# Hybrid decoder step on one core: key-norm reciprocals as a power on GpSimd, output blocks of 96, 96 and 72 rows

## The chip, the cores and the metric

The kernel runs on one core of one Trainium2 chip. The metric is the device time of one execution in microseconds (us). The engines are TensorE (PE in the profile, its weight loads PEld), VectorE (DVE), ScalarE (ACT), GpSimd (POOL) and SyncE (SP), which here only starts transfers. Transfers start on the queues of SP and of ACT.

## The reference

One layer of a hybrid decoder, for 256 new prompt positions and 8 decoding samples, 264 columns in all, in float32:

```
x = x + 0.5 * swiglu(rmsnorm(x, n1), f1g, f1u, f1d)
proj = rmsnorm(x, nm) @ w_in
mixed = [window attention with sinks and relative bias | RWKV-7 time mixing]
x = x + mixed @ w_out
x = x + 0.5 * swiglu(rmsnorm(x, n2), f2g, f2u, f2d)
y = rmsnorm(x, final_norm)
```

The model width is 2048, the feed-forward width 5504. The RWKV half has 16 heads of 64. In it, each head's key direction is normalised before the scan over time:

```
kk = k * k_k
kk = kk / max(sqrt(sum(kk * kk over the head)), 1e-12)
```

It also returns the window keys and values, the RWKV state and the shift columns of both kinds of sequence.

## The kernel before

**Layout.** Activations lie with 128 model columns on the partitions and the 264 sequence columns on the free axis, so x is 16 blocks of 128x264. Weights come from memory in chunks of 128x512 or 128x384.

**The split product.** Every weight product (`gemm`, lines 144 to 158) is made in three passes of a reduced float32 form: `chunk` (133 to 142) loads a chunk into `raw` (six buffers, SP's queue), ScalarE writes its rounded part `hi` (line 140), VectorE the rest, `lo = raw - hi` (line 141, through the helper on line 67), each in a ring of four. For each of the chunk's blocks TensorE makes hi x hi, hi x lo and lo x hi. TensorE thus waits for a chunk's `hi` and `lo`, and ScalarE and VectorE wait for a free place in the ring.

**Stages.** `first_ffn` (312), then `mixing` (363), then `second_ffn` (996). In the mixing stage the input projection's blocks run in the order of SEQ (line 48). Each RWKV pair of heads (eight pairs, two to a batch) spawns a generator `prep` (437), each batch a generator `chain` (562), each attention block `attend`; `tick` (91) advances all of them once after every chunk of a product, and `pause(n)` lets n ticks go by. So the small work of the mixing stage is interleaved with the big products in the program's order. The framework then orders each engine's instructions with a planner that prices each instruction and keeps a timeline (`schedule_with_timeline_sim=True`, line 1181); on the chip each engine takes its own instructions in that order.

**The norm of the keys** (447 to 464). `kk` is the scaled key of a pair (128 partitions, two heads), `b` its square. After `pause(PW[0])` a product with `bo`, a matrix of ones over each head's 64 partitions, sums the squares into PSUM, `nps`. VectorE takes the reciprocal of `nps` into `b` (453). Then come the scan of the decays (455), GpSimd's memset of the first column of `W` (456), the exponentials, a copy to `wc`, and after `pause(PW[1])` one VectorE operation makes `b = min(b, 1e24) * kk` (463). From `b` follow the pair's operands `BK` and `XD`, and with them the batch's chain.

**The end** (1028 to 1072). The last product's squares are summed over the model axis. y is written in two forms. Blocks 0 to 7 and 12 to 15 go out as they lie, 128 partitions by 264 columns each, into `yT`, after a product with the reciprocal root spread over all partitions. Blocks 8 to 11 are turned by TensorE, so that the 264 sequence positions lie on partitions in three groups of 88 rows, 512 wide; ScalarE and VectorE scale them by a reciprocal root per row (`rt`) and they go into `yt`. `sums`, `turns` and `spread` are TensorE's parts, held in the order of the program. The stores of `yt` are two on SP and one on ACT; of `yT` three on SP and two on ACT.

Of the kernel before, what the change touches and what calls it, by code (L numbers as in the profile page):

```python
# [7 lines left out]
F32 = mybir.dt.float32  # L8
F32R = mybir.dt.float32r
AF = mybir.ActivationFunctionType  # L10
ALU = mybir.AluOpType
AX = mybir.AxisListType

P = 128
NP = 256
NB = 8
T = NP + NB
D = 2048
# [24 lines left out]
PX = (1, 2, 1, 1)  # L43
DL = 2
XA = 3
ALPHA = math.exp(-0.5)
LKV = 26
SEQ = [('b', 0), ('b', 1), ('b', 2), ('kv', 0), ('kv', 1), ('kv', 2), ('kv', 3), ('q', 0), ('q', 1), ('q', 2), ('q', 3), ('b', 3), ('q', 4), ('q', 5), ('q', 6), ('q', 7)]
# [7 lines left out]
def body(tc, I, O):  # L56
    nc = tc.nc
    V, A, G, TE, SP = nc.vector, nc.scalar, nc.gpsimd, nc.tensor, nc.sync
# [7 lines left out]
    def tt(e, out, a, b, op):  # L66
        return e.tensor_tensor(out=out, in0=a, in1=b, op=op)  # L67
# [4 lines left out]
    def ts(e, out, a, s1, op0, s2=None, op1=None):  # L72
        k = {} if op1 is None else dict(op1=op1)
        e.tensor_scalar(out=out, in0=a, scalar1=s1, scalar2=s2, op0=op0, **k)

    def act(out, in_, f, **k):
        return A.activation(out=out, in_=in_, func=f, **k)  # L77

    def bc(ap, shape):
        return ap.broadcast_to(list(shape))  # L80

    def mm(out, lhsT, rhs, start=True, stop=True, **k):
        return TE.matmul(out, lhsT, rhs, start=start, stop=stop, **k)  # L83
# [24 lines left out]
    with ExitStack() as ctx:  # L108
        cp = ctx.enter_context(tc.tile_pool(name="cp", bufs=1))
# [52 lines left out]
        ss = cp.tile([P, NSH, NB], F32, name="ss")  # L162
        ones = cp.tile([P, P], F32, name="ones")
        G.memset(ones, 1.0)
        eps = cp.tile([P, 2], F32, name="eps")
        G.memset(eps[:, 0:1], 1e-5)
        G.memset(eps[:, 1:2], 64e-5)
        act(eps[:, 0:1], eps[:, 0:1], AF.Copy)
# [199 lines left out]
        def mixing_body(mx, n2, n3, XD, XR):  # L368
# [11 lines left out]
            ident, bo, cm = C[:, CID:CID + P], C[:, CBO:CBO + P], C[:, CCM:CCM + P]  # L380
            msk = C[:, CMK:CMK + P]
            keep = fix((P, NP), "keep")
# [54 lines left out]
            def prep(p, bt, k, xrr, xk, xv):  # L437
# [9 lines left out]
                kk, b = tmp(), tmp()  # L447
# [2 lines left out]
                yield from pause(PW[0])  # L450
                nps = mp()
                mm(nps[:, :T], bo, b)
                V.reciprocal(b, nps[:, :T])
                W, Wi = tmp((P, 4, 65)), tmp((P, 4, 64))
                V.tensor_tensor_scan(Wi.rearrange("p c t -> p (c t)"), keep, sg[:, :NP], 0.0, ALU.mult, ALU.add)
                G.memset(W[:, :, 0:1], 1.0)
                act(W[:, :, 1:65], Wi, AF.Exp, scale=-ALPHA)
                act(Wi, Wi, AF.Exp, scale=ALPHA)
# [24 lines left out]
                vp = mp()  # L483
# [18 lines left out]
                for c in range(4):  # L502
                    for h in range(2):
                        r = HALF[h]
                        mm(gps[h][:, c * P:(c + 1) * P], BK[r, c, h:h + 2, :], KR[r, 0:2, c, :])
                for h in range(2):
# [3 lines left out]
                    for blk in range(2):  # L510
                        x = blk * 32
# [6 lines left out]
                kp = mp()  # L518
# [17 lines left out]
                for i in range(NB):  # L536
                    c, g = i // 2, i % 2
                    for h in range(2):
                        r, o = HALF[h], HALF[1 - h]
# [371 lines left out]
            for kind, i in SEQ:  # L911
                if kind == "b":
                    bt = newbatch(i)
                    for k in range(BATCH[i]):
                        p = bt.p0 + k
                        x = [shifted(2 + 3 * p + j, tmp()) for j in range(3)]
# [5 lines left out]
                elif kind == "kv":  # L922
                    w, p = i // 2, i % 2
# [11 lines left out]
                else:  # L935
                    ps = win(LKV + 4 + i)
                    q = ob[i]
# [8 lines left out]
            xr = blk("x1", 8) + blk("x0", 8)  # L946
            for o in range(XA):
                SP.dma_start(xr[o], xsp[o])
# [15 lines left out]
            for pi, ks in enumerate(PASS):  # L964
# [3 lines left out]
                to = pairs(*(late + [xs4[1], more] if ks[0] > 7 else xs4[:1]))  # L968
# [11 lines left out]
                for o in range(KD):  # L980
                    if not pi and o + XA < KD:
                        behind(SP.dma_start(xr[o + XA], xsp[o + XA]))
                    ps = acc()
# [12 lines left out]
        def second_ffn(n3, xr, XR):  # L996
            fin = Norm(VGF, most=3)

            def load(k):
                if k >= CH:  # L1000
                    n3.split(xr[k], True)

            with tc.tile_pool(name="f2", bufs=1) as fp:
                cur[0] = (fp, NH)
                ys = [fp.tile([P, 4, T], F32, tag="y", bufs=4, name=uid("y")) for _ in range(4)]
                rt = fp.tile([88, 48], F32, name="rt")
                sq = fp.tile([P, NQ, T], F32, name="sq")
                n3.sq = fin.sq = [sq[:, j] for j in range(NQ)]

                def nxt(o):  # L1010
                    fin.square(xr[o])
                    if o == 0:
                        act(rt[:, 7:8], fin.sums[0][0][0:88, 0:1], AF.Sqrt)
                    act(ys[o // 4][:, o % 4], xr[o], AF.Copy, scale=vc(VGF + o))

                def last(ps, x):
                    a, b = slice(0, 176), slice(176, T)
                    q = fin.free.pop(0)
                    u, w = fin.sums[0]
                    tt(G, w, w, u, ALU.add)  # L1020
                    stt(x[:, a], ps[:, a], 0.5, x[:, a], ALU.mult, ALU.add)
                    stt(x[:, b], ps[:, b], 0.5, x[:, b], ALU.mult, ALU.add)
                    tt(V, q[:, b], x[:, b], x[:, b], ALU.mult)
                    act(q[:, a], x[:, a], AF.Square)
                    fin.sums[0] = [w, q]
                    act(ys[3][:, 3], x, AF.Copy, scale=vc(VGF + KD - 1))

                side = dec_state(fp, XR)
                ffn(n3, xr, I["gu2"], I["dn2"], nxt, load, None, side, end=last)
                assert next(side, side) is side  # L1030
                p, ident = fin.sums[0], C[:, CID:CID + P]
                assert len(p) == 2
                sm, rp, again = mp(), mp(), acc()
                turn, keep = [mp(), acc(), mp()], tc.keep_in_program_order
                todo = [(j, o) for j in range(3) for o in range(4)]

                def sums(i):
                    for j in range(3):
                        keep(mm(sm[0:88, j:j + 1], p[i][:, j * 88:j * 88 + 88], ones[:, 0:1], i + j == 0, i == 1, skip_group_check=True))

                def turns(n):
                    for _ in range(n):
                        j, o = todo.pop(0)
                        keep(TE.transpose(turn[j][0:88, o * P:o * P + P], ys[2][:, o, j * 88:j * 88 + 88], ident))

                def spread(to):
                    for j in range(3):
                        keep(TE.transpose(to[:, j * 88:j * 88 + 88], bc(rt[:, j:j + 1], (88, P)), ident[0:88, 0:88]))

                sums(0)  # L1050
                turns(5)
                sums(1)
                act(rt[:, 0:3], sm[0:88, 0:3], AF.Sqrt, scale=1.0 / D, bias=eps[0:88, 0:1])
                V.reciprocal(rt[:, 0:3], rt[:, 0:3])
                yt = fp.tile([88, 3, 512], F32, name="yt")
                rb = tmp()
                turns(4)
                spread(again)
                spread(rp)
                turns(3)  # L1060
                act(yt[:, 0], turn[0][0:88, :], AF.Copy, scale=rt[:, 0:1])
                ts(V, yt[:, 1], turn[1][0:88, :], rt[:, 1:2], ALU.mult)
                SP.dma_start(O["yt"][:, 0], yt[:, 0])
                SP.dma_start(O["yt"][:, 1], yt[:, 1])
                A.copy(rb, again[:, :T])
                act(yt[:, 2], turn[2][0:88, :], AF.Copy, scale=rt[:, 2:3])
                A.dma_start(O["yt"][:, 2], yt[:, 2])
                for e, q, o, n, d, r in ((V, SP, 0, 1, 0, rp[:, :T]), (V, SP, 1, 3, 1, rp[:, :T]), (G, A, 4, 3, 4, rb),
                                         (V, SP, 12, 4, 8, rp[:, :T]), (V, A, 7, 1, 7, rp[:, :T])):
                    y = ys[o // 4][:, o % 4:o % 4 + n]  # L1070
                    tt(e, y, y, bc(r.unsqueeze(1), (P, n, T)), ALU.mult)
                    q.dma_start(O["yT"][:, d:d + n, :], y)

        xsp = [dp.tile([P, T], F32, tag=f"xsp{o}", name=f"xsp{o}") for o in range(KD)]
# [4 lines left out]
        with tc.tile_pool(name="dx", bufs=1) as dx:  # L1079
# [2 lines left out]
            second_ffn(n3, mixing(n2, n3, XD, XR), XR)  # L1082


OUTS = dict(yT=(P, 12, T), yt=(88, 3, 512), kp=(2, P, P), vp=(2, P, P), ks=(NB, P, 256), vs=(NB, P, 256),
            wkvp=(NPAIR, P, 64), wkvs=(P, 64, 64), sh=(P, NSH, NB + 1))


# [69 lines left out]

def unlay(o):
    y = o["yT"].transpose(2, 1, 0).reshape(T, 12 * P)  # L1160
    y = np.concatenate([y[:, :8 * P], o["yt"].transpose(1, 0, 2).reshape(T, 512), y[:, 8 * P:]], 1)
    kv = lambda x: np.ascontiguousarray(x.reshape(2, 2, 64, P).transpose(3, 0, 1, 2)).reshape(1, 1, P, 4, 64)
    wp = o["wkvp"].reshape(16, 64, 64).transpose(0, 2, 1)[None, None]
    ws = o["wkvs"].reshape(2, 8, NB, 64, 64).transpose(2, 1, 0, 3, 4).reshape(1, NB, 16, 64, 64)
    sh = np.empty((9, NSH * P), np.float32)
    sh[:, _sources()[:NSH * P] - 1536] = o["sh"].transpose(2, 1, 0).reshape(9, NSH * P)
    c = np.ascontiguousarray
    return (c(y[None, :NP]), c(y[NP:, None]), kv(o["kp"]), kv(o["vp"]), c(wp), c(sh[None, None, 0]),
            c(o["ks"].reshape(1, NB, P, 4, 64)), c(o["vs"].reshape(1, NB, P, 4, 64)), c(ws), c(sh[None, 1:]))
# [15 lines left out]
```

## Time and profile before

| | |
|---|---|
| median of 3 runs | 1936.75 us (1935.41 to 1936.86) |
| the profiled execution's own time | 1936.05 us |
| its span, first to last instruction | 1934.2 us |
| TensorE busy | 1920.2 us, 99% |
| VectorE busy | 1311.8 us, 68% |
| ScalarE busy | 1027.9 us, 53% |
| GpSimd busy | 258.2 us, 13% |
| bytes moved | 357.28 MB, mean 185 GB/s |
| granted TensorE clock, mean | 0.999 |

The page of a profile lists the busy time of each engine, the chain of work that ended last (each step followed back to what released it), and groups of equal instructions: line, engine, operation, output and inputs, shape, count, then busy time, mean duration in ns, and the engine's idle time just before them with what ended it. A view by windows gives each engine's busy time in a stretch, with the number of instructions in brackets, and then the granted clock, the share of the 16 DMA engines' time and GB/s. A timeline has start, duration, engine and instruction; rows of the same kind that follow each other are merged, with their count. Line 67 is the helper for two-input operations, line 70 for operations with a scalar and a tensor, line 74 for operations with scalars, line 77 for ScalarE's functions, line 83 for products; so groups are told apart by the names of their tiles.

### The profile page before, as it was taken

The numbers are of one execution on the slowest core, as the hardware profiler recorded it, in microseconds if no ns is written. First come the engines' busy times: TensorE is split into PE (matmuls) and PEld (weight loads), VectorE is DVE, ScalarE is ACT, GpSimd is POOL, SyncE is SP. The second block draws the span as 40 slices with busy tenths as digits, with TensorE's granted clock in tenths as the row PEclk, the third lists the DMA queues.
The fourth block names the chain that finished last, engine by engine and source line by source line (L and its number), as shares of the span: only waits on it lengthen the run. The fifth ranks groups of instructions, "written<-read, shape, count | busy, mean of one in ns | idle before, by whom it ended". The sixth has DMA issues, their size and how long they took to land.

```text
span 1934.2 us, 45549 instructions
## 1 busy us (share of the span) xinstructions
PE 1920.2 (99%) x17171; PEld 1896.7 (98%) x17171; DVE 1311.8 (68%) x2622; ACT 1027.9 (53%) x2041; POOL 258.2 (13%) x376
## 2 busy tenths in 40 slices
PE   9999999999999999999999999999999999999998
PEld 9999999999999999999989999999999999999997
DVE  5865555655556568889888977866666666666655
ACT  5644444444444457676667555644444444444446
POOL 0401101011010113222101100300101001010012
PEclk9999999999999999999999999999999999999999
DMA  7566666665666668655645756666666666666664
GB/s 241 177 192 196 185 195 194 184 191 176 191 183 181 186 183 241 173 165 156 173 124 159 211 155 184 175 188 188 188 195 194 185 193 189 195 195 185 192 181 149
DMA packets 218599, 357.28 MB, mean 185 GB/s; under 512 B 33522, under 2 KB 71938, under 8 KB 218378
## 3 DMA queue, kind: packets, MB, share of 16 engines
q1 hardware_dynamic: 212054, 346.39, 61.0%
q10 hardware_dynamic: 6323, 7.98, 1.3%
q8 instruction: 134, 2.20, 0.5%
q14 instruction: 88, 0.71, 0.1%
HBM read 346.67 MB, written 9.69 MB: 184 GB/s over the span
## 4 chain that ended last, share of the span: by engine, by line
PE 98%; ACT 1%; DVE 0%; DMA 0%; issue 0%; DVEq 0%
PE acc L83 90%; PE m L83 7%; DMA x<-in_x 0%; ACT hi L140 0%; ACT t L77 0%; ACT BT L532 0%; ACT kr L523 0%; PE m L527 0%; PE m L808 0%; PE m L485 0%; DVE y L67 0%; PE m L728 0%; ACT x L953 0%; PE m L809 0%; PE m L810 0%
## 5 line engine op out<-in xcount | busy, mean ns | idle before, releaser
L67 DVE TENSOR_TENSOR lo<-raw,hi 128x512 fp32r<-128x512 f32 (+1 forms) x1288 | 875.3, 683 | 512.2 <-ACT hi L140 490.3
L140 ACT CAST hi<-raw 128x512 fp32r<-128x512 f32 (+1 forms) x1288 | 777.0, 606 | 815.9 <-PE acc L83 742.7
L83 PE MATMUL acc<-x,hi 128*128 128x264 f32 x4840 | 894.5, 286 | 1.0 <-ACT hi L140 1.0
L83 PEld LDWEIGHTS acc<-x,hi 128*128 128x128 f32 x4840 | 750.3, 189 | 6.3 <-issue 2.5
L83 PE MATMUL acc<-x,lo 128*128 128x264 f32 x2420 | 690.8, 286 | 0.2 <-DVE lo L67 0.2
L83 PE MATMUL acc<-h,hi 128*128 128x264 f32 x2752 | 495.0, 284 | 0.0
L83 PEld LDWEIGHTS acc<-x,lo 128*128 128x128 f32 x2420 | 457.2, 189 | 2.2 <-DVE lo L67 0.6
L83 PEld LDWEIGHTS acc<-h,hi 128*128 128x128 f32 x2752 | 424.4, 189 | 0.0
L83 PE MATMUL acc<-h,lo 128*128 128x264 f32 x1376 | 387.8, 284 | 0.0
L83 PEld LDWEIGHTS acc<-h,lo 128*128 128x128 f32 x1376 | 259.2, 189 | 0.0
L67 POOL TENSOR_TENSOR t<-t,t 128x264 f32<-128x264 f32 x74 | 79.9, 1079 | 1096.0 <-DVE t L67 949.8
L83 PE MATMUL acc<-y,hi 128*128 128x264 f32 x648 | 122.7, 284 | 0.0
L83 PE MATMUL acc<-o,hi 128*128 128x264 f32 x648 | 120.1, 284 | 0.0
L83 PE MATMUL acc<-kv,hi 128*128 128x264 f32 x582 | 109.7, 285 | 0.0
L83 PEld LDWEIGHTS acc<-y,hi 128*128 128x128 f32 x648 | 101.2, 189 | 0.1
L83 PEld LDWEIGHTS acc<-o,hi 128*128 128x128 f32 x648 | 100.1, 189 | 0.0
L70 DVE SCALAR_TENSOR_TENSOR x<-acc,x 128x264 f32<-128x264 f32 (+1 forms) x193 | 81.2, 425 | 24.3 <-PE acc L83 23.4
L83 PE MATMUL acc<-y,lo 128*128 128x264 f32 x324 | 92.0, 284 | 0.0
L83 PE MATMUL acc<-o,lo 128*128 128x264 f32 x324 | 92.0, 284 | 0.0
L83 PEld LDWEIGHTS acc<-kv,hi 128*128 128x128 f32 x582 | 89.9, 189 | 0.1
L67 DVE TENSOR_TENSOR t<-acc,t 128x264 f32<-128x264 f32 x156 | 67.4, 432 | 32.8 <-PE acc L83 32.8
L83 PE MATMUL acc<-kv,lo 128*128 128x264 f32 x291 | 82.9, 285 | 0.0
(309 smaller groups left out, 1596.1 us busy)
## 6 DMA issues: line engine op xcount, KB each, us to landing
raw<-in_gu SPq DMA_DIRECT2D x688, 256.0 KB, 3.3
raw<-in_dn SPq DMA_DIRECT2D x224, 256.0 KB, 2.8
raw<-in_win SPq DMA_DIRECT2D x152, 256.0 KB, 3.5
raw<-in_dn SPq DMA_DIRECT2D x160, 192.0 KB, 2.7
raw<-in_wout SPq DMA_DIRECT2D x64, 256.0 KB, 3.5
xsp<-x ACTq DMA_DIRECT2D x16, 132.0 KB, 3.9
x<-xsp SPq DMA_DIRECT2D x16, 132.0 KB, 4.5
ld<-in_sT SPq DMA_DIRECT2D x16, 128.0 KB, 3.1
```

What stands on the lines that cost most here:

```text
L67: return e.tensor_tensor(out=out, in0=a, in1=b, op=op)
L70: return V.scalar_tensor_tensor(out=out, in0=a, scalar=s, in1=b, op0=op0, op1=op1)
L83: return TE.matmul(out, lhsT, rhs, start=start, stop=stop, **k)
L140: A.copy(hi[:, :w], raw[:, :w])
```

## The change

The reciprocal of the summed squares is no longer taken by VectorE from PSUM. ScalarE copies the sums out of PSUM into `b`, and GpSimd raises `b` to the power of minus one, element by element, with the exponent read from a third column of `eps` that is spread over the 264 columns. The third column is set once at the start, by a memset on GpSimd.

At the end, the turned blocks are cut into groups of 96, 96 and 72 rows in place of three of 88. The root and the reciprocal per row are made in two steps, one for the first two groups and one for the third. `yt` in memory becomes 264 x 512. The fully laid out blocks are stored as 0, 1 to 3, 4 to 7 and 12 to 15 in place of 0, 1 to 3, 4 to 6, 12 to 15 and 7; GpSimd multiplies blocks 4 to 7, four of them. Queues: SP has the first two row groups, block 0 and blocks 4 to 7; ACT has the third row group, blocks 1 to 3 and 12 to 15.

```diff
+ROWS = ((0, 96), (96, 96), (192, 72))
...
-        eps = cp.tile([P, 2], F32, name="eps")
+        eps = cp.tile([P, 3], F32, name="eps")
+        G.memset(eps[:, 2:3], -1.0)
...
                 mm(nps[:, :T], bo, b)
-                V.reciprocal(b, nps[:, :T])
+                A.copy(b, nps[:, :T])
+                tt(G, b, b, bc(eps[:, 2:3], (P, T)), ALU.pow)
...
                 def spread(to):
-                    for j in range(3):
-                        keep(TE.transpose(to[:, j * 88:j * 88 + 88], bc(rt[:, j:j + 1], (88, P)), ident[0:88, 0:88]))
+                    for j, (c, n) in enumerate(ROWS):
+                        keep(TE.transpose(to[:, c:c + n], bc(rt[0:n, j:j + 1], (n, P)), ident[0:n, 0:n]))
...
-                act(rt[:, 0:3], sm[0:88, 0:3], AF.Sqrt, scale=1.0 / D, bias=eps[0:88, 0:1])
-                V.reciprocal(rt[:, 0:3], rt[:, 0:3])
-                yt = fp.tile([88, 3, 512], F32, name="yt")
+                for c, n in ((slice(0, 2), ROWS[0][1]), (slice(2, 3), ROWS[2][1])):
+                    act(rt[0:n, c], sm[0:n, c], AF.Sqrt, scale=1.0 / D, bias=eps[0:n, 0:1])
+                    V.reciprocal(rt[0:n, c], rt[0:n, c])
+                yt = fp.tile([P, 3, 512], F32, name="yt")
...
-                for e, q, o, n, d, r in ((V, SP, 0, 1, 0, rp[:, :T]), (V, SP, 1, 3, 1, rp[:, :T]), (G, A, 4, 3, 4, rb),
-                                         (V, SP, 12, 4, 8, rp[:, :T]), (V, A, 7, 1, 7, rp[:, :T])):
+                for e, q, o, n, r in ((V, SP, 0, 1, rp[:, :T]), (V, A, 1, 3, rp[:, :T]), (G, SP, 4, 4, rb), (V, A, 12, 4, rp[:, :T])):
                     y = ys[o // 4][:, o % 4:o % 4 + n]
                     tt(e, y, y, bc(r.unsqueeze(1), (P, n, T)), ALU.mult)
+                    d = min(o, 8)
                     q.dma_start(O["yT"][:, d:d + n, :], y)
```

`sums` and `turns` take their groups of rows from ROWS in the same way.

More of the change, by code (lines that the diff above doesn't have):

```diff
@@ L1005, in second_ffn @@
                 ys = [fp.tile([P, 4, T], F32, tag="y", bufs=4, name=uid("y")) for _ in range(4)]
-                rt = fp.tile([88, 48], F32, name="rt")
+                rt = fp.tile([P, 48], F32, name="rt")
                 sq = fp.tile([P, NQ, T], F32, name="sq")
@@ L1012, in nxt @@
                     if o == 0:
-                        act(rt[:, 7:8], fin.sums[0][0][0:88, 0:1], AF.Sqrt)
+                        act(rt[:, 7:8], fin.sums[0][0][:, 0:1], AF.Sqrt)
                     act(ys[o // 4][:, o % 4], xr[o], AF.Copy, scale=vc(VGF + o))
@@ L1037, in sums, with turns @@
                 def sums(i):
-                    for j in range(3):
-                        keep(mm(sm[0:88, j:j + 1], p[i][:, j * 88:j * 88 + 88], ones[:, 0:1], i + j == 0, i == 1, skip_group_check=True))
-                def turns(n):
-                    for _ in range(n):
+                    for j, (c, n) in enumerate(ROWS):
+                        keep(mm(sm[0:n, j:j + 1], p[i][:, c:c + n], ones[:, 0:1], i + j == 0, i == 1, skip_group_check=True))
+                def turns(k):
+                    for _ in range(k):
                         j, o = todo.pop(0)
-                        keep(TE.transpose(turn[j][0:88, o * P:o * P + P], ys[2][:, o, j * 88:j * 88 + 88], ident))
+                        c, n = ROWS[j]
+                        keep(TE.transpose(turn[j][0:n, o * P:o * P + P], ys[2][:, o, c:c + n], ident))
                 def spread(to):
-                    for j in range(3):
-                        keep(TE.transpose(to[:, j * 88:j * 88 + 88], bc(rt[:, j:j + 1], (88, P)), ident[0:88, 0:88]))
+                    for j, (c, n) in enumerate(ROWS):
+                        keep(TE.transpose(to[:, c:c + n], bc(rt[0:n, j:j + 1], (n, P)), ident[0:n, 0:n]))
                 sums(0)
@@ L1060, in second_ffn @@
                 turns(3)
[L1061 to L1064, printed above, removed]
+                ends = [(rt[0:n, j:j + 1], turn[j][0:n, :], yt[0:n, j], O["yt"][c:c + n]) for j, (c, n) in enumerate(ROWS)]
+                r, x, y, o = ends[0]
+                act(y, x, AF.Copy, scale=r)
+                SP.dma_start(o, y)
+                r, x, y, o = ends[1]
+                ts(V, y, x, r, ALU.mult)
+                SP.dma_start(o, y)
                 A.copy(rb, again[:, :T])
-                act(yt[:, 2], turn[2][0:88, :], AF.Copy, scale=rt[:, 2:3])
-                A.dma_start(O["yt"][:, 2], yt[:, 2])
-                for e, q, o, n, d, r in ((V, SP, 0, 1, 0, rp[:, :T]), (V, SP, 1, 3, 1, rp[:, :T]), (G, A, 4, 3, 4, rb),
-                                         (V, SP, 12, 4, 8, rp[:, :T]), (V, A, 7, 1, 7, rp[:, :T])):
+                r, x, y, o = ends[2]
+                act(y, x, AF.Copy, scale=r)
+                A.dma_start(o, y)
+                for e, q, o, n, r in ((V, SP, 0, 1, rp[:, :T]), (V, A, 1, 3, rp[:, :T]), (G, SP, 4, 4, rb), (V, A, 12, 4, rp[:, :T])):
                     y = ys[o // 4][:, o % 4:o % 4 + n]
                     tt(e, y, y, bc(r.unsqueeze(1), (P, n, T)), ALU.mult)
+                    d = min(o, 8)
                     q.dma_start(O["yT"][:, d:d + n, :], y)
@@ L1082, in body @@
             second_ffn(n3, mixing(n2, n3, XD, XR), XR)
-OUTS = dict(yT=(P, 12, T), yt=(88, 3, 512), kp=(2, P, P), vp=(2, P, P), ks=(NB, P, 256), vs=(NB, P, 256),
+OUTS = dict(yT=(P, 12, T), yt=(T, 512), kp=(2, P, P), vp=(2, P, P), ks=(NB, P, 256), vs=(NB, P, 256),
             wkvp=(NPAIR, P, 64), wkvs=(P, 64, 64), sh=(P, NSH, NB + 1))
@@ L1160, in unlay @@
     y = o["yT"].transpose(2, 1, 0).reshape(T, 12 * P)
-    y = np.concatenate([y[:, :8 * P], o["yt"].transpose(1, 0, 2).reshape(T, 512), y[:, 8 * P:]], 1)
+    y = np.concatenate([y[:, :8 * P], o["yt"], y[:, 8 * P:]], 1)
     kv = lambda x: np.ascontiguousarray(x.reshape(2, 2, 64, P).transpose(3, 0, 1, 2)).reshape(1, 1, P, 4, 64)
```

## The prediction

> **What bounds the kernel now.** I read the page's engine shares first, then the chain of work that ended last, then the costliest groups.
>
> ```profile
> span 1934.2 us, 45549 instructions
> PE 1920.2 (99%) x17171; PEld 1896.7 (98%) x17171; DVE 1311.8 (68%) x2622; ACT 1027.9 (53%) x2041; POOL 258.2 (13%) x376
> PE 98%; ACT 1%; DVE 0%; DMA 0%; issue 0%; DVEq 0%
> L67 DVE TENSOR_TENSOR lo<-raw,hi 128x512 fp32r<-128x512 f32 (+1 forms) x1288 | 875.3, 683 | 512.2 <-ACT hi L140 490.3
> L140 ACT CAST hi<-raw 128x512 fp32r<-128x512 f32 (+1 forms) x1288 | 777.0, 606 | 815.9 <-PE acc L83 742.7
> ```
>
> TensorE is the bound: it is busy for 1920.2 of 1934.2 us and holds 98% of the chain. ScalarE (`hi`) and VectorE (`lo`) split each weight chunk for it, and the 742.7 us in which ScalarE waits for TensorE to give back a chunk say that the split normally runs ahead. The change lies in two other places: in the mixing stage, where the key norms are made, and in the stores of the end. So next come the window of the eight pairs, and the line of the reciprocal.
>
> ```profile
> core 0: us, PE busy (x) PEld busy (x) DVE busy (x) ACT busy (x) POOL busy (x), PEclk, DMA share, GB/s
> 785.00:1050.00 265.00, 262.97 (x3063) 247.91 (x3063) 234.75 (x658) 173.52 (x445) 51.87 (x129) 1.00 0.56 157
> L453 DVE RECIPROCAL t<-m x8: 1794/1795/1808, 787.4 to 1036.2; 128x264 f32<-128x264 f32 x8
> ```
>
> Even here TensorE is idle for only 265.00 - 262.97 = 2.0 us, at a full granted clock. VectorE is the second engine: 234.75 of 265 us, 89%. GpSimd has room on average, 51.87 us.
>
> **The change part by part, the reciprocal first.** It removes 8 reciprocals of 1.80 us from VectorE, 14.4 us. Did they cost TensorE anything? The timelines of VectorE and of TensorE around the first:
>
> ```profile
> 786.52 0.69 DVE L67 TENSOR_TENSOR lo<-raw,hi 128x512 fp32r<-128x512 f32 x1
> 787.40 1.81 DVE L453 RECIPROCAL t<-m 128x264 f32<-128x264 f32 x1 [0.18 <-PE m L83]
> 789.41 0.68 DVE L67 TENSOR_TENSOR lo<-raw,hi 128x512 fp32r<-128x512 f32 x1
> 790.00 0.43 DVE L70 SCALAR_TENSOR_TENSOR t<-t,t 128x264 f32<-128x264 f32 x1
> 787.32 0.41 PE L83 MATMUL acc<-x,hi 128*128 128x264 f32 x2
> 787.68 0.41 PE L83 MATMUL acc<-x,hi 128*128 128x264 f32 x2
> 788.06 0.40 PE L83 MATMUL acc<-x,hi 128*128 128x264 f32 x2
> 788.42 0.40 PE L83 MATMUL acc<-x,hi 128*128 128x264 f32 x2
> ```
>
> During the reciprocal TensorE starts a group of three products every 0.36 to 0.38 us, without a gap. The ring of four `hi`/`lo` chunks covers it: a chunk is four such groups, 4 x 0.36 = 1.44 us. Removing the reciprocal is therefore worth nothing on the path; the most that all of this stage could give back is the 2.0 us above.
>
> In its place come a ScalarE copy out of PSUM and a power on GpSimd, on 128x264. The nearest rows:
>
> ```profile
> L77 ACT ACTIVATE t<-m 128x264 f32<-128x264 f32 x8 | 3.2, 400 | 1.0 <-PE m L83 1.0
> ACT hi L140 <- PE acc L83: 44.0, 46, 3.1
> L67 POOL TENSOR_TENSOR t<-t,t 128x264 f32<-128x264 f32 x74 | 79.9, 1079 | 1096.0 <-DVE t L67 949.8 <-ACT hi L140 123.4 <-ACT t L77 20.8
> L74 POOL TENSOR_SCALAR t<-t 128x264 f32<-128x264 f32 x8 | 4.0, 502 | 16.8 <-ACT t L77 16.8
> L74 POOL TENSOR_SCALAR XD<-t 128x8 f32<-128x8 f32 x8 | 2.5, 307 | 2.2 <-ACT t L77 1.8 <-DMA ld<-in_bias 0.3
> L460 POOL COPY wc<-t 128x4 f32<-128x4 f32 x8 | 3.2, 402 | 7.7 <-ACT t L77 7.7
> ```
>
> The copy: 8 x 0.40 = 3.2 us of ScalarE, hidden by the 44.0 us that it waits for TensorE (second row, between 780 and 1050 us). I set it to nothing; without that cover it would be 3.2 us. While it waits for the norm's matmul, `hi` casts stand behind it on ScalarE, as `lo` subtractions stood behind the reciprocal before.
>
> The power: no row shows one. **Bounds.** Below: 1.08 us, what GpSimd takes for a plain two-input operation of this size (from there the change is free). Above: the dearest price per column that GpSimd shows, 402 ns for 4 columns, 100 ns each, x 264 = 26.5 us. **The value between:** the scalar rows at 264 and at 8 columns differ by 195 ns for 256 columns and two arithmetic steps (multiply, add), which makes 0.38 ns per column and step, 0.10 us for 264 columns. A power in full float32 is a logarithm, a product and an exponential; I assume 80 such steps (two polynomials, splitting, special cases), an assumption that no row fixes. 80 x 0.10 + 0.3 (the fixed part) = **8.3 us**. It lies nearer to the arithmetic rows than to the copy, which is nearly all fixed cost.
>
> The GPSIMD Engine Reference of the Trainium skill (3.1, Elementwise) puts a loop of three or more operations per element at roughly three operations a cycle, at 1.2 GHz; by that page's figures 80 steps would be 80 / 3 x 264 / 1.2 GHz = 5.9 us, an estimate, and the total some 1954 us instead of the one below. No run here shows a power.
>
> **What the power blocks** matters more than where it stands. Timelines of VectorE and of GpSimd at another place:
>
> ```profile
> 77.89 0.42 DVE L67 TENSOR_TENSOR t<-t,t 128x264 f32<-128x264 f32 x1
> 78.23 1.24 DVE L67 TENSOR_TENSOR lo<-raw,hi 128x512 fp32r<-128x512 f32 x1
> 79.40 0.77 DVE L67 TENSOR_TENSOR t<-t,t 128x264 f32<-128x264 f32 x2
> 78.05 0.88 POOL L67 TENSOR_TENSOR t<-t,t 128x264 f32<-128x264 f32 x1 [2.10 <-DVE t L67]
> ```
>
> A `lo` of 0.69 us takes 1.24 us here, 0.55 more. It starts at 78.23, when GpSimd has been at work since 78.05, and ends 0.54 us after GpSimd's end at 78.93: about what remains of its work if it could not run until then. I read this as VectorE's two-input operation standing still until GpSimd's is over. So a power of 8.3 us holds up every `lo` for its whole length, wherever the consumer (the minimum with 1e24, at 790.00 above, 2.6 us after the reciprocal began) is put. The consumer alone, without that block, would wait 0.4 + 8.3 - 2.6 = 6.1 us and hold the `lo`s behind it in VectorE's queue.
>
> **The stall.** Three finished chunks ahead of TensorE are 3 x 1.44 = 4.3 us of its work. After the power one `lo` (0.69) must come. Loss per pair 8.3 + 0.7 - 4.3 = 4.7 us, eight times 37.4 us. Cross-check by VectorE's budget: 234.75 - 14.4 + 8 x 8.3 = 286.8 us for a stretch of 265, so at least 22 us longer. I take 37.4: TensorE, otherwise full, has nothing with which to catch up. Bounds: nothing for a power up to 3.6 us (3.6 + 0.7 = 4.3); 8 x (26.5 + 0.7 - 4.3) = 183 us at the ceiling. Behind the power on GpSimd stand the first column of W, the copies to `shc` and `XD`; three `pj` buffers and 35.5 us between pairs (1036.2 - 787.4, over 7) leave them time.
>
> **The end.** The windows of the stores, and the steps ahead of them:
>
> ```profile
> 1925.80:1926.40 0.60, 0.00 (x0) 0.00 (x0) 0.60 (x2) 0.20 (x1) 0.60 (x1) 1.00 0.65 137
> 1926.40:1927.00 0.60, 0.00 (x0) 0.00 (x0) 0.60 (x1) 0.00 (x0) 0.60 (x1) 1.00 0.82 284
> 1927.00:1931.00 4.00, 0.00 (x0) 0.00 (x0) 0.81 (x2) 0.00 (x0) 0.16 (x1) 0.76 1.01 373
> 1931.00:1931.50 0.50, 0.00 (x0) 0.00 (x0) 0.00 (x0) 0.00 (x0) 0.00 (x0) 0.50 0.94 368
> 1931.50:1932.00 0.50, 0.00 (x0) 0.00 (x0) 0.00 (x0) 0.00 (x0) 0.00 (x0) 0.50 0.67 262
> 1932.00:1932.50 0.50, 0.00 (x0) 0.00 (x0) 0.00 (x0) 0.00 (x0) 0.00 (x0) 0.50 0.48 175
> 1923.77 0.26 ACT L77 ACTIVATE rt<-m,eps 88x3 f32<-88x3 f32 x1 [0.32 <-PE m L83]
> 1924.06 0.17 DVE L1054 RECIPROCAL rt<-rt 88x3 f32<-88x3 f32 x1 [0.94 <-ACT rt L77]
> 1924.79 0.49 PE L1044 MATMUL m<-C,y 128*88 128x128 f32 x3
> 1925.29 1.87 POOL L67 TENSOR_TENSOR y<-y,t 128x792 f32<-128x792 f32 x1 [3.70 <-ACT t L1065]
> 1927.19 2.01 ACTq L1072 DMA_DIRECT2D out_yT<-y  x2
> ```
>
> The DMA engines are full from 1927 to 1931 (share 1.01); bytes end this stage, and their sum stays. Short of full they lack 0.6 x (0.35 + 0.18) + 0.5 x (0.06 + 0.33 + 0.52) = 0.77 us, the most that other rows and queues can give. Against it, the root and the reciprocal become two each: the second root and reciprocal put VectorE's block some 0.2 us later. GpSimd's product grows to four blocks, 1.87 x 4 / 3 = 2.49 us, and ends 0.6 us later, near 1927.8; its store then goes out about when the last one does now, with the engines still full. I take -0.5 + 0.2 = **-0.3 us**, between -0.8 and +0.8 (GpSimd's 0.6 and the 0.2 both exposed). The new memset of -1 at the start is hidden by the first loads.
>
> DMA: Bandwidth & Descriptors of the Trainium skill (Why a DMA increments its semaphore by 16 and not by 1) gives a transfer the largest number of engines up to 16 that divides its slowest dimension: 11 for 88 rows, 16 for 96, 12 for 72. By it the fullest engines drop from 24 rows of 2 KB to 18, an estimated 0.5 us at the 373 GB/s shown; the shares under 1 agree.
>
> **Sum.** The profiled execution took 1936.05 us, 0.7 below the median of 1936.75. 1936.05 + 37.4 - 0.3 = 1973.2; against the median **1974 us**, some 1.9% slower. A difference under 0.2%, 3.9 us, counts as none.
>
> **The rivals.**
> - *Not slower: the power fits under the chunks.* Place: the `lo` ring at each pair; price nothing, up to a power of 3.6 us. It would also hold for a longer one if the block were not for the whole instruction and the planner put other work ahead of the consumer. For it: GpSimd's 1.08 us and 89% on VectorE that falls by 14.4 us. Against: a function in software instead of one operation. 1936.75 - 0.3 = 1936.4.
> - *Far slower: the power costs near the ceiling.* From about 15 us on, the loss is 11 us a pair and more; at 26.5 us 183, and 2119 us. GpSimd then also becomes late for itself: with 26.5 us per pair and its own work, pairs that follow within less wait in its queue. For it: the power's step count is unknown. Against: the arithmetic rows.
> - *Faster: the freed 14.4 us reach TensorE.* The 2.0 us of idle time and 0.8 at the end together are 2.8 us, 0.14%: 1934. Even whole it would not pass 0.2%.
>
> **How the numbers follow.** Forecast (a power of about 4.5 to 15 us) 0.53; ceiling 0.18; not slower 0.26; faster 0.03. The not-slower case and the power's that lose under 3.9 us give same 0.26; slower 0.71; faster 0.03. The range takes in the free power and the ceiling: 1935.5 to 2120. The likeliest alone: powers of 5.5 and 13 us lose 8 x 1.9 = 15 and 8 x 9.4 = 75 us, so 1952 to 2012.
>
> **What would show it.** In the changed kernel's groups the power's own mean: 8.3 us right, under 3.6 the first rival, over 15 the second. `lo` operations that end with the power, several us long or after as long a gap, show the block. TensorE's idle time between 785 and the end of the eighth pair should grow from 2 to near 39 us, and the stage before 785 and the second feed-forward should keep their lengths. In the end, DMA share near 1 from the first store, and less than 8.9 us from TensorE's last product (1925.28) to the span's end (1934.2). If a power is long and TensorE stays full, the block or the planner's order is misread.

## The result, and the profile after

The changed kernel takes **2214.97 us** (median of 4 runs, 2214.35 to 2220.62) against 1936.8 us: a ratio of 1.1447, 95% interval 1.1432 to 1.1461. The forecast was 1974 us, in a range up to 2120. The direction was right; the loss is 278 us and not 37. Of the experiments below, 1 to 3 and the 24 columns of 10 rest on 2 to 11 executions, the others on one each; the kernel before took 1935.7 to 1935.9 us beside them. The changed kernel's own four lie 6 us apart, so a few us between two of these kernels count for nothing.

The page of the changed kernel, first the engine shares and the chain, then its groups:

```profile
span 2212.6 us, 45579 instructions
PE 1966.5 (89%) x17171; PEld 1931.5 (87%) x17171; DVE 1317.7 (60%) x2614; ACT 1035.7 (47%) x2052; POOL 584.7 (26%) x385
PE 79%; POOL 14%; DVE 3%; ACT 2%; DMA 1%; issue 1%; SPq 0%; POOLq 0%; ACTq 0%; DVEq 0%
L68 POOL TENSOR_TENSOR t<-t,eps 128x264 f32<-128x264 f32 x8 | 340.1, 42512 | 12.8 <-ACT t L455 9.5
L84 PE MATMUL m<-t,C 128*128 128x264 f32 (+1 forms) x32 | 14.2, 534 | 176.2 <-POOL t L68 176.2
L71 DVE SCALAR_TENSOR_TENSOR t<-t,t 128x264 f32<-128x264 f32 x16 | 8.0, 501 | 173.3 <-POOL t L68 173.0
```

A power takes 42.5 us where I had set 8.3, eight of them 340.1 us. GpSimd, which was not in the chain at all, now has 14% of it. TensorE stands 176.2 us ahead of a small product and VectorE 173.3 us ahead of the power's reader, both ended by GpSimd. (The helpers' lines are one higher than before, because of the new line 46, later lines by two or more.)

Where the time went, by windows of both kernels, that before and then the changed one (columns as in the prediction). The mixing stage lies between 757 and 1150 us before, and between 757 and 1430 after:

```profile
757.00:1150.00 393.00, 390.26 (x4450) 368.50 (x4449) 334.74 (x944) 252.25 (x639) 69.78 (x177) 1.00 0.59 167
```

```profile
0.00:757.00 757.00, 754.69 (x6267) 753.90 (x6268) 464.56 (x788) 383.38 (x693) 96.92 (x104) 1.00 0.65 193
757.00:1430.00 673.00, 437.58 (x4458) 404.38 (x4457) 342.46 (x938) 261.07 (x652) 395.45 (x185) 0.79 0.34 98
1430.00:2212.60 782.60, 774.20 (x6452) 773.24 (x6450) 510.70 (x889) 391.28 (x708) 92.34 (x96) 1.00 0.63 186
```

The feed-forward stages on either side keep their lengths. The mixing stage grows by 673 - 393 = 280 us with the same products on TensorE (4458 against 4450). Of these, TensorE is idle for 673.00 - 437.58 = 235.4 us, against 2.7 before: 233 us. The other 437.58 - 390.26 = 47 us are products that take longer: the granted clock of the stage is 0.79, against 1.00 before. Around the first standstill, with 4 products in a microsecond at a clock of 0.50 and 11 at 1.00:

```profile
816.60:817.60 1.00, 0.30 (x3) 0.09 (x1) 0.26 (x2) 0.62 (x1) 1.00 (x1) 1.00 0.62 178
819.60:820.60 1.00, 0.00 (x0) 0.00 (x0) 0.00 (x0) 0.00 (x0) 1.00 (x1) 0.54 0.47 168
820.60:822.00 1.40, 0.00 (x0) 0.00 (x0) 0.00 (x0) 0.00 (x0) 1.40 (x1) 0.50 0.08 29
835.00:836.00 1.00, 1.00 (x4) 0.79 (x3) 0.79 (x3) 0.50 (x2) 0.52 (x3) 0.50 0.00 0
837.00:838.00 1.00, 1.00 (x11) 1.00 (x10) 0.14 (x1) 0.95 (x3) 0.47 (x3) 1.00 0.50 131
```

The last product starts at 816.6. Some three microseconds later the granted clock falls to 0.50, and it comes back only three to four microseconds after TensorE has gone on at 833.0. Later standstills of this trace have the same two clocks, but other delays: up to some 5 us to fall and 3 to 8 us to rise. "TensorE: Matmul & The Clock Gate" of the Trainium skill (What's actually happening) gives about 3.4 us of idleness to fall to half the clock and as much of work to rise again. This trace agrees in size, not as a fixed delay: the first fall comes 2.8 us after the last product's end.

How the standstill comes about is seen in the timelines of the changed kernel around the first power, of GpSimd, ScalarE, VectorE and TensorE:

```profile
787.81 42.47 POOL L68 TENSOR_TENSOR t<-t,eps 128x264 f32<-128x264 f32 x1 [1.34 <-ACT t L455]
787.35 0.38 ACT L455 COPY t<-m 128x264 f32<-128x264 f32 x1 [0.91 <-PE m L84]
788.37 0.69 DVE L68 TENSOR_TENSOR lo<-raw,hi 128x512 fp32r<-128x512 f32 x1
799.65 0.43 DVE L68 TENSOR_TENSOR pj<-acc,rs 128x264 f32<-128x264 f32 x1 [0.22 <-PE acc L84]
817.46 0.69 DVE L68 TENSOR_TENSOR lo<-raw,hi 128x512 fp32r<-128x512 f32 x1 [0.74 <-ACT hi L141]
830.31 0.90 DVE L71 SCALAR_TENSOR_TENSOR t<-t,t 128x264 f32<-128x264 f32 x2 [12.16 <-POOL t L68]
831.25 0.61 ACT L78 ACTIVATE t<-t,less,half 128x264 f32<-128x264 f32 x1 [13.82 <-DVE t L71]
831.76 0.49 ACT L78 ACTIVATE t<-pj,vec 128x256 f32<-128x256 f32 x1
832.66 0.29 POOL L68 TENSOR_TENSOR t<-XD 128x16 f32<-128x16 f32 x1
833.01 1.29 PE L84 MATMUL m<-t,C 128*128 128x280 f32 x2 [16.11 <-POOL t L68]
```

Three readings, and two of them are against my prediction. The `lo` subtractions go on at 0.69 us while the power runs, so nothing holds them for its length. The planner has put some 29 us of big products ahead (TensorE works until 816.9). But then each engine stands at an instruction of the pair: VectorE at the reader of the power, ScalarE at the step after it, TensorE at the product with the bonus sums. And ready work is behind: ScalarE's `t<-pj,vec` of the next block reads a `pj` that VectorE wrote long before, and starts only at 831.76, behind the pair's step (the last `pj` before the standstill is that of 799.65). What releases TensorE is not the power itself but a small product of GpSimd, `t<-XD` at 832.66: it stands behind the power in GpSimd's queue, and it also reads what the pair makes of the power's result.

### The profile page after: what moved, and what is told of

It is laid out like the page before. It is cut to its first block, busy times and chain, and to the rows that moved or that the text cites. A ratio compares the mean times of both kernels' runs of the same rounds, so it can differ in the third digit from the quotient of the medians.

```text
span 2212.6 us, 45579 instructions
## 1 busy us (share of the span) xinstructions
PE 1966.5 (89%) x17171; PEld 1931.5 (87%) x17171; DVE 1317.7 (60%) x2614; ACT 1035.7 (47%) x2052; POOL 584.7 (26%) x385
## 4 chain that ended last, share of the span: by engine, by line
PE 79%; POOL 14%; DVE 3%; ACT 2%; DMA 1%; issue 1%; SPq 0%; POOLq 0%; ACTq 0%; DVEq 0%
PE acc L84 73%; POOL t L68 14%; PE m L84 6%; ACT t L78 1%; DMA Xt<-sa 1%; DVE Xt L68 0%; DVE st L68 0%; DVE t L71 0%; DVE t L804 0%; ACT hi L141 0%; SPq L576 0%; DVE bk L68 0%; DVE lo L68 0%; DVE t L68 0%; DMA x<-in_x 0%
## 5 line engine op out<-in xcount | busy, mean ns | idle before, releaser
L84 PEld LDWEIGHTS acc<-x,hi 128*128 128x128 f32 x4840 | 759.7, 191 | 49.5 <-POOL x L68 28.4
L84 PEld LDWEIGHTS acc<-x,lo 128*128 128x128 f32 x2420 | 462.6, 191 | 2.7 <-DVE lo L68 1.8
L68 POOL TENSOR_TENSOR t<-t,eps 128x264 f32<-128x264 f32 x8 | 340.1, 42512 | 12.8 <-ACT t L455 9.5
L84 PE MATMUL m<-t,C 128*128 128x264 f32 (+1 forms) x32 | 14.2, 534 | 176.2 <-POOL t L68 176.2
L84 PEld LDWEIGHTS m<-t,C 128*128 128x128 f32 x32 | 6.2, 241 | 177.7 <-POOL t L68 177.6
L71 DVE SCALAR_TENSOR_TENSOR t<-t,t 128x264 f32<-128x264 f32 x16 | 8.0, 501 | 173.3 <-POOL t L68 173.0
L78 ACT ACTIVATE t<-t,less,half 128x264 f32<-128x264 f32 x8 | 4.9, 607 | 190.9 <-DVE t L71 190.8
```

Source lines behind the costliest of these rows:

```text
L71: return V.scalar_tensor_tensor(out=out, in0=a, scalar=s, in1=b, op0=op0, op1=op1)
```

## The experiments

**1. The end alone.** Which part costs?

```diff
-                A.copy(b, nps[:, :T])
-                tt(G, b, b, bc(eps[:, 2:3], (P, T)), ALU.pow)
+                V.reciprocal(b, nps[:, :T])
```

> The changed kernel with VectorE's reciprocal put back; the new row groups, stores and queues stay. If the whole loss is the power's, this takes 1936.4 us (my term for the end, -0.3, range -0.8 to +0.8), and the stage between 785 and 1050 us looks as before. Rival: if the end had a part in the loss, it is over 1938.

Measured: 1935.65 us against 1935.72, ratio 0.9999 (0.999 to 1.0008). No difference that can be told. The two profiles still show the end shorter. Last products of the kernel with the new end alone, then the end's windows and the same product in the changed kernel:

```profile
1926.20 0.49 PE L1047 MATMUL m<-C,y 128*72 128x128 f32 x3
```

```profile
2203.77 0.49 PE L1048 MATMUL m<-C,y 128*72 128x128 f32 x3
2204.26 2.42 POOL L68 TENSOR_TENSOR y<-y,t 128x1056 f32<-128x1056 f32 x1 [3.69 <-ACT t L1073]
2204.80:2205.40 0.60, 0.00 (x0) 0.00 (x0) 0.60 (x2) 0.18 (x1) 0.60 (x1) 1.00 0.97 270
2205.40:2206.00 0.60, 0.00 (x0) 0.00 (x0) 0.60 (x1) 0.00 (x0) 0.60 (x1) 0.58 0.94 294
2210.50:2211.00 0.50, 0.00 (x0) 0.00 (x0) 0.00 (x0) 0.00 (x0) 0.00 (x0) 0.50 0.53 211
```

From the last product to the end of the span: 8.9 us before, 1935.1 - 1926.7 = 8.4 us with the end alone, 2212.6 - 2204.3 = 8.3 us in the changed kernel. The DMA engines are at 0.97 from the first stores on, against 0.65 before. So the end gains about 0.5 us in the profiles, and the differences between runs hide it.

**2. The power alone.**

```diff
-                V.reciprocal(b, nps[:, :T])
+                A.copy(b, nps[:, :T])
+                tt(G, b, b, bc(eps[:, 2:3], (P, T)), ALU.pow)
```

> The kernel before with only the copy and the power in place of the reciprocal; the end is the old one. If the two parts are independent: 2215.0 + 0.3 = 2215.3 us, within 3 us. Rival: the planner's order of the mixing stage depends on the rest of the program, and it is off by tens of us.

Measured: 2218.61 us, ratio 1.146 (1.1439 to 1.1481). The whole loss is the power's. The median lies 0.3 us outside the 3 us that I had allowed, but the changed kernel's own runs go up to 2220.62 us, so nothing can be made of the 3.6 us between the two.

**3. The route without the power's length.**

```diff
-        G.memset(eps[:, 2:3], -1.0)
+        G.memset(eps[:, 2:3], 1e-9)
...
-                tt(G, b, b, bc(eps[:, 2:3], (P, T)), ALU.pow)
+                tt(G, b, b, bc(eps[:, 2:3], (P, T)), ALU.mult)
```

> The changed kernel with a multiplication by 1e-9 on GpSimd in place of the power, so the reciprocal is left out and the keys' norms are wrong; copy, engine, operands, shapes and waits stay. The GpSimd operation should take 0.75 to 1.1 us in place of 42.5. If the power's length is everything: 1936.4 us, as with the reciprocal on VectorE. Rival: the route itself (a hop over ScalarE and GpSimd ahead of the pair's operands, other work of GpSimd behind it) costs something: 1938 to 1945.

Measured: 1941.65 us, ratio 1.0027 (1.0016 to 1.0038); the GpSimd operation takes 0.63 to 1.06 us. The rival holds here: even with a short operation the route costs 6 us. TensorE's idle and waiting times in this kernel don't put it down to one wait, and I leave open which.

**4. The same power, read by nobody.** Two causes can stand behind the picture above: the pair waits for the power's *result*, or other work waits *behind the power in GpSimd's queue*.

```diff
-                A.copy(b, nps[:, :T])
-                tt(G, b, b, bc(eps[:, 2:3], (P, T)), ALU.pow)
+                raw = tmp()
+                A.copy(raw, nps[:, :T])
+                V.reciprocal(b, nps[:, :T])
+                tt(G, raw, raw, bc(eps[:, 2:3], (P, T)), ALU.pow)
```

> The changed kernel with VectorE's reciprocal back for the result, and beside it the copy and the power into a temporary that nobody reads (it takes one of the 16 places of the ring of temporaries while the power runs). GpSimd is occupied as long as before, but no one needs the power's result. Theory A (what stops the kernel is GpSimd's queue: copies to shc and XD and small products that stand behind a power of 42.5 us): most of the loss stays, 2150 to 2215 us. Theory B (the wait for the power's result, the pair's own chain): the loss goes, under 1960 us. In between, both have a share.

Measured: 2196.99 us. That looks like theory A. The standstill has another place, though; timeline of VectorE:

```profile
817.63 0.69 DVE L68 TENSOR_TENSOR lo<-raw,hi 128x512 fp32r<-128x512 f32 x1 [0.74 <-ACT hi L141]
830.95 1.11 DVE L68 TENSOR_TENSOR pj<-acc,rs 128x264 f32<-128x264 f32 x3 [12.63 <-POOL shc L425]
```

VectorE now stands before `pj`, since GpSimd's copies out of the three buffers `pj` are behind the power. That is the smaller part, as TensorE's longest waits show:

```profile
PE m L84 <- POOL t L68: 96.8, 5, 28.4
PE acc L84 <- DVE pj L68: 36.2, 3, 15.2
PE acc L84 <- POOL x L68: 27.8, 1, 27.8
```

Most of TensorE's wait is for GpSimd's small product `t<-XD`, which also stands behind the power: after the second one it ends at 887.35 us, and TensorE goes on at 887.40.

**5. One of GpSimd's copies on ScalarE.**

```diff
-                G.tensor_copy(shc[:, t, :], pj[:, NP:NP + NB + 1])
+                A.copy(shc[:, t, :], pj[:, NP:NP + NB + 1])
```

> The changed kernel with one group of GpSimd's copies on ScalarE: those of the projection's last columns to shc, which free the three buffers pj. In the changed kernel TensorE works 29.3 us on after the first power begins, five blocks of the input projection, and pj is written three times, then both stand. Theory A1 (the ring pj is what runs out): TensorE works on for the whole first power, and the total falls by 50 us or more. Theory A2 (the pair's small products on GpSimd behind the power hold TensorE in its order) or B (the power's result): within 20 us of 2215.

Measured: 2216.85 us. Theory A1 falls for the changed kernel: with the result awaited, and with the pair's other work still behind the power, freeing `pj` is worth nothing. A2 and B are both left.

**6. GpSimd with the power and nothing else.** In the mixing stage every other GpSimd instruction goes to VectorE or ScalarE, for example:

```diff
-                ts(G, sg, sg, 0.5, ALU.mult, 0.5, ALU.add)
+                ts(V, sg, sg, 0.5, ALU.mult, 0.5, ALU.add)
...
-                    G.tensor_copy(XD[:, i, p, :], src[:, NP:T])
+                    A.copy(XD[:, i, p, :], src[:, NP:T])
```

> The changed kernel with the mixing stage's other GpSimd work on VectorE and ScalarE, so that GpSimd does the eight powers there and nothing else. Theory A (GpSimd's queue): the loss shrinks to what eight powers in a row need, 787 + 340 + some 112 us from the last norm to the end of the stage = 1239 in place of 1150, so 2025 to 2060 us. Theory B (the result is awaited in the pair's chain, whose next norm comes only after it): 2180 to 2215 us.

Measured: 2214.91 us, unchanged. TensorE's waits in this kernel:

```profile
PE m L84 <- DVE t L68: 171.6, 7, 45.7
PE acc L84 <- DVE t L68: 42.9, 2, 39.7
```

With the queue clear, the result alone holds everything as long. So each of the two, the queue here and the result in experiment 4, looks innocent when it alone is removed.

**7. Both removed at once.** The edits of 4 and 6 together.

> Both edits together: the mixing stage's other GpSimd work on VectorE and ScalarE, VectorE's reciprocal back for the result, and the power into a temporary that nobody reads. Each alone kept nearly the whole loss (2215 and 2197 us). Theory C (the queue and the result are two separate blocks in parallel, either of which costs the whole): with both gone 1936 to 1960 us. Theory D (a common third thing, the ring of 16 temporaries of which the power holds one, or the power's traffic): over 2050 us.

Measured: **1952.49 us**. GpSimd still runs all eight powers, 42.4 to 42.6 us each, back to back:

```profile
L68 POOL TENSOR_TENSOR t<-t,eps x8: 42431/42450/42588, 788.7 to 1085.8; 128x264 f32<-128x264 f32 x8
785.00:1160.00 375.00, 360.67 (x4176) 338.33 (x4176) 318.92 (x966) 242.83 (x683) 339.59 (x8) 0.99 0.52 156
```

TensorE is busy for 360.67 of 375 us beside 339.59 us of powers. Theory C holds: two blocks in parallel, either of which costs nearly the whole. The power's own traffic and the load on GpSimd cost at most the 17 us that are left; the small work that moved to VectorE and ScalarE may have a part in them, which no run separates.

**8. More buffers, and their control.** Does the ring of 16 temporaries keep the next pair's norm from starting?

```diff
-CH, NRAW, NHL = 4, 6, 4
+CH, NRAW, NHL = 4, 4, 4
...
-NH, NQ, NT, NLD = 16, 8, 16, 6
+NH, NQ, NT, NLD = 16, 8, 23, 6
...
-NGM, NKR, NUV, NTT, NBT = 10, 5, 3, 2, 5
+NGM, NKR, NUV, NTT, NBT = 8, 5, 3, 2, 5
```

> The changed kernel with 23 in place of 16 buffers in the ring of temporaries (room from the rings of raw, 4 for 6, and of gm, 8 for 10). A pair holds some ten of them from its projection to its operands, so with 16 the second pair behind a waiting one can't get its norm's buffers. Theory R (the ring keeps the next pair's norm from starting, so that powers and pair chains take turns): the powers move together, the loss falls by 60 us or more, to 2030 to 2155 us. Theory O (the order of small products in TensorE's queue, which the ring does not change): within 25 us of 2215.

> The same rings (23 temporaries, 4 raw, 8 gm) with VectorE's reciprocal in place of the copy and the power: the control for the run before. Both theories: 1936 to 1950 us; if the smaller rings cost more than that, the run before is read against this one.

Measured: 2222.19 us with the power, 1941.03 with the reciprocal. The rings themselves cost 5 us; the loss stays at 281. Theory R falls. ScalarE's `t<-pj,vec` too still starts behind the pair's step (836.36 us, after 835.84), so it was not a temporary that it had waited for.

**9. The reader 43 us later.** If the wait is paid in the engines' orders, moving the reader back in the order must help. The edit is that of 6, the rings of 8, and

```diff
-PW = (2, 1, 3, 3, 9)
+PW = (2, 30, 3, 3, 9)
```

> GpSimd does the powers alone in the mixing stage (the rest on VectorE and ScalarE), the rings are 23 temporaries, 4 raw, 8 gm, and the pair's generator lets 30 ticks of the big products go by between the power and its first reader, not 1 (a tick is a chunk, 1.44 us: 43 us). The result stays the power's. Theory C (the reader and all that the pair issues after it stand in VectorE's, ScalarE's and TensorE's order ahead of the next blocks' work, and that is where the whole wait is paid): the powers follow each other with little between, and the loss falls to what eight in a row need, 787 + 340 + 112 us = 1239 for the end of the stage, 2025 to 2085 us in all. Rival (something else makes powers and chains take turns): 2150 to 2220 us.

Measured: **2046.55 us**, 168 us less than in experiment 6, with every key norm still from the power. Its powers and TensorE's waits for the pair:

```profile
L68 POOL TENSOR_TENSOR t<-t,eps x8: 42432/42448/43521, 794.0 to 1136.5; 128x264 f32<-128x264 f32 x8
PE m L84 <- DVE t L68: 17.2, 2, 14.3
```

The eight begin between 794.0 and 1136.5 us, six of them back to back and two after a gap of 43.85 us, and end near 1179. TensorE's wait for the pair falls from 171.6 us to 17.2. That fits theory C, and the time lies in its range; but the powers are not quite eight in a row, and what sets the 111 us that are left was not worked out. Two more limits: the larger rings changed together with the reader's place (in experiment 8 they were worth nothing, but there GpSimd's queue was not clear), and no run has a late reader with the queue as it was.

**10. Shorter powers.** 132 columns, then 24, the other columns by VectorE's reciprocal:

```diff
-                A.copy(b, nps[:, :T])
-                tt(G, b, b, bc(eps[:, 2:3], (P, T)), ALU.pow)
+                A.copy(b[:, :132], nps[:, :132])
+                tt(G, b[:, :132], b[:, :132], bc(eps[:, 2:3], (P, 132)), ALU.pow)
+                V.reciprocal(b[:, 132:], nps[:, 132:T])
```

> The changed kernel with the power on columns 0 to 131 and VectorE's reciprocal on the other 132. If the power costs by the column, it takes 21.3 us. The loss per pair was 279 / 8 = 34.9 us for 42.5, so 7.6 us are covered; if that cover stays, 8 x (21.3 - 7.6) = 110 us and 2046 us. Rival: the cover is the planner's filling of about 26 us of products behind the first power; then the loss is near nothing, under 1970 us.

> The changed kernel with the power on 24 columns and VectorE's reciprocal on the other 240. At 21.44 us for 132 columns and 42.47 for 264 (159 ns a column, 0.4 us fixed) the power takes 4.2 us. The loss at the two lengths, 112 and 279 us, is a line 8 x (x - 7.4 us): nothing is left at 4.2 us but what the route cost with a multiplication, 6 us: 1936 to 1942 us. Rival, by the prediction's own sum with a block of every lo: 8 x (4.2 + 0.7 - 4.3) = 5 us more, 1941 to 1947.

The groups of the two kernels:

```profile
L68 POOL TENSOR_TENSOR t<-t,eps 128x132 f32<-128x132 f32 x8 | 171.7, 21458 | 9.3 <-ACT t L455 9.3
```

```profile
L68 POOL TENSOR_TENSOR t<-t,eps 128x24 f32<-128x24 f32 x8 | 34.7, 4334 | 8.8 <-ACT t L455 8.7
```

Measured: 2048.32 us and 1947.36 us (1.0057, 1.004 to 1.0074). A power costs by the column: (42.5 - 21.5) / 132 = 0.16 us. The loss at 132 columns is 113 us, where 110 were expected. At 24 columns the line 8 x (x - 7.4), drawn through the two longer powers, leaves nothing but the route's 6 us; the loss is 11.6 us. So the line does not reach down, and a power of 4.3 us is not free. The rival's 1947 us is missed by only 0.4, but its cause is not there: no `lo` beside these powers takes more than 0.72 us. What costs the 11.6 us stays open.

## Why the prediction was right or wrong, step by step

- **TensorE bounds, the removed reciprocals are worth nothing:** nothing speaks against it. With the route kept and the power's length gone (experiment 3) the kernel doesn't gain; it loses 6 us. No run takes the reciprocals out without the route.
- **The copy on ScalarE is hidden:** its length is right, 0.38 us, set at 0.40. That the whole route is free was wrong, by 6 us with a multiplication and 11.6 with a power of 4.3; whether the copy has a part in this is not shown.
- **The power at 8.3 us, at most 26.5:** the first step that failed, and the larger one. It is 42.5 us. The 0.10 us per arithmetic step may stand, but 80 steps was an assumption: at that price the power is worth some 420. And the ceiling was none. A copy of four columns bounds the fixed cost of an instruction; no row of one function bounds another function from above. By the prediction's own formula 42.5 us would have made 8 x (42.5 + 0.7 - 4.3) = 311 us, 2248: nearer than 1974, for a wrong reason. (8 x 4.7 is 37.6 and not 37.4, which changes nothing.)
- **A power holds every `lo` for its whole length:** wrong. The `lo`s beside it take 0.69 us; with the powers back to back (experiment 7) none of 152 took more than 0.70. What stops TensorE is the consumer's wait, which the prediction had as the smaller effect (6.1 us), and beside it GpSimd's queue.
- **"Wherever the consumer is put":** wrong once GpSimd's queue is clear: with the pair's later work 43 us back in the order, and larger rings, the time is 168 us less (experiment 9). With the queue as it was, the place alone could hardly have helped, for a result that nobody reads still leaves 2197 us (experiment 4). The sum's cover of 4.3 us a pair was mis-sized too: the planner had put some 29 us of big products behind the start of the first power, and 11 to 16 us behind those of six others.
- **Three `pj` buffers leave time behind the power:** wrong at this length. Experiment 4 shows VectorE standing 12.63 us for `shc`, and TensorE 96.8 us for `t<-XD`, a small product that the prediction's list of work behind the power leaves out. GpSimd's queue is a second block, hidden beside the first.
- **TensorE's clock:** a term that the prediction did not have. It counted only idle time; the products after the standstills ran at half the clock and took 47 us longer, a sixth of the loss.
- **The end, -0.3 us between -0.8 and +0.8:** the right size, -0.5 by the profiles, and too small to tell in the medians. GpSimd's four blocks took 2.42 us (2.49 set), and the early DMA share rose as listed.
- **The rivals:** "far slower" named the right cause, a power whose step count is unknown, and the wrong mechanism for its price; it did say that GpSimd becomes late for itself. The range ended at 2120 because the ceiling did.

## What to carry to other kernels

An operation that no row of the trace shows can't be bounded by rows of other operations: measure it alone on a few columns, or treat its price as open upward. When an instruction grows long, it can block twice: those who read its result, and those who stand behind it in its queue. Removing either alone may show next to nothing, so remove both before calling either harmless. And a wait on an engine that takes its instructions in order is paid by all the ready work behind it, so look at where the reader stands in the order, not only at how long the producer takes.

## What the runs showed of the hardware

A power on GpSimd costs 159 ns per column: 4.2 to 4.6 us for 24, 21.5 for 132, 42.5 for 264 columns of float32 on 128 partitions, while a multiplication by the same spread column takes 0.63 to 1.06 us for 264. By the three operations a cycle that "GPSIMD Engine Reference" of the Trainium skill gives (3.1, Elementwise), 159 ns at 1.2 GHz would be some 570 operations per column, an estimate, where I had supposed 80.

Where the power holds VectorE at all, it does so only at its start. In the changed kernel a `lo` that begins 0.12 us after a power takes 1.12 us (another, 0.23 us after one, 0.94), one before it 0.68, and VectorE's two-input operations after it run at their usual length, while the power has 40 us to go; VectorE, then GpSimd:

```profile
907.84 0.68 DVE L68 TENSOR_TENSOR lo<-raw,hi 128x512 fp32r<-128x512 f32 x1
908.82 1.12 DVE L68 TENSOR_TENSOR lo<-raw,hi 128x512 fp32r<-128x512 f32 x1
909.86 0.22 DVE L68 TENSOR_TENSOR st<-X,Xt 128x72 f32<-128x72 f32 x1
908.70 42.53 POOL L68 TENSOR_TENSOR t<-t,eps 128x264 f32<-128x264 f32 x1
```

"SBUF — State Buffer" of the Trainium skill (Who interferes with whom) calls the pair of ports that the two engines share an exclusive lock, and has a VectorE instruction with two inputs in SBUF contend with a GpSimd instruction that reads SBUF. The prediction's row of 1.24 us fits a lock for the whole of a plain two-input operation; for the power that doesn't hold, where the block ends about half a microsecond into the 42.5. Why it ends there, no run here shows.
